# Eight PSUM banks, the input gates and the first head pair's third tile: a change of order at the start of a hybrid decoder step

## The chip, the cores and the metric

The kernel runs on one core of one Trainium2 chip. The metric is device time in microseconds (us), the median of three runs. Engines are named as in the profile: PE (TensorE matmul), PEld (its weight load), DVE (VectorE), ACT (ScalarE), POOL (GpSimd), SP (SyncE, which here issues every transfer; SPq is its queue). L193 is line 193 of the kernel.

## The reference, cut to what matters

One layer of a decoder on 512 prompt tokens and 8x8 sample tokens, 576 columns in all, with 1024 features:

```
h  = rmsnorm(x, norm1_g);  z = h @ w_in          # w_in: 1024 x 5896
li = z[M_I:M_F] + m_i_bias                       # input gate of the mLSTM, 4 heads
lf = log_sigmoid(z[M_F:M_END] + m_f_bias)        # its forget gate
hm = mlstm_chunked(q, k, v, li, lf, ...)         # q, k: conv + silu of z; v, o: z
xm = zr + (prev - zr) * r_mix                    # token shift of the RWKV columns
r, kr, vr = xm[0:512], xm[512:1024], xm[1024:1536]   # then decay, a and gate loras
yr = rwkv7_scan(r, decay, k, v, -kk, kk * a, S0)
x += (gates[0] * (hm @ w_branch_m) + gates[1] * (yr @ w_branch_r)) @ w_out
x += (gelu(conv(h2 @ f_up[:, 0])) * (h2 @ f_up[:, 1])) @ f_down
x += sigmoid(rmsnorm(x) @ ple_gate_w) * (pe @ ple_proj);  y = rmsnorm(x)
```

## The kernel before, in words

Features lie on the 128 partitions, tokens along the free axis; the 576 tokens are worked in two halves (hf 0 and 1) of HF = 288. An output tile of a projection is 128 features x 576 tokens: two PSUM banks, one for each half. Each float32 operand is split into a high and a low part, and each k of the 8 input tiles takes three matmuls (high x high, high x low, low x high), so half an output tile is 24 matmuls of 128x288, all issued at L193. Weights come through `wload` (L158 on) in pieces of four k: SP loads a piece into one of RB = 6 buffers `wr`, ACT casts it (L169, `wh`), DVE subtracts (L170, `wl`) into one of WB = 4 pairs of buffers. A new piece therefore waits for the matmuls of the piece four earlier, and its load for the subtraction of the piece six earlier.

The eight PSUM banks are handed out by tag through `bank`: three "d", two "r", one each of "s", "c", "m". A bank is given out again in turn, and the next user waits until the last reader of the one before is done.

A scheduler orders the instructions of every engine when the kernel is built; each engine then runs its own list strictly in that order. The source's order enters as priority: a step that is written later yields to those before it.

At the start, three tiles of w_in, the `lead` (12 and 13, the RWKV loras, and 0, the r of the first pair), are multiplied with unnormalised x, and their banks are scaled by the first norm's row factors `rsr` (half 0 at L425, half 1 at L429) when they are read out (`evac_pad`, L355). With the factors known, the normalised input is made half by half (`norm_half`: DVE L268, ACT L269, DVE or POOL L270; tiles xa0h to xa7l, sixteen in all). Then come the input and forget gates ("if", L458, 16 matmuls a half because the two parts of the weights lie side by side) and w_in's tile 4, the k of the first pair. What follows is a list of steps, `PLAN`: x, a, d, b, s and c are the stages of one pair of RWKV heads (projections and token shift; decay and matrices; inverses of 16x16 blocks on DVE; chunk matrices; samples; output), m is an mLSTM head, g a gate tile. Step x0 uses tiles 0, 4 and 8; tiles 0 and 4 are there by then, and tile 8, the v of the first pair, is an ordinary `dense` with two banks of tag "d". Before the first step stands `mlstm_rows()`: it reads the gates' banks (ACT L975 and L976, DVE L977 and L978, once for each half), and computes the rows of the mLSTM from them (ACT L979 to L981, DVE L982 to L1017), up to a small matmul at L1020 and transposes at L1024.

Each of r_tile's outputs passes through a buffer `zr` of two; one of the two is first used for a block of zeros, `zscr`, which SP writes to four scratch tensors in DRAM (L547, scr0q to scr1t), so that the second tile that needs a `zr` (tile 8) waits for these transfers. At the very start four matmuls on zeros (L394) run before any input is there; ACT's first copy writes a column of their operand `warm` (L391).

Of the kernel before, what the change touches and what calls it, by code (L numbers as in the profile page):

```python
# [7 lines left out]
F32 = mybir.dt.float32  # L8
# [7 lines left out]
P = 128  # L16
# [6 lines left out]
KD = D // P  # L23
# [4 lines left out]
KSC = 128.0 ** -0.5  # L28
DEC = math.exp(-0.5)

PLAN = "x0 a0 d0 x1 b0 a1 d1 s0 c0 g0 m0 b1 g1 x2 a2 d2 s1 c1 m1 g2 b2 x3 a3 d3 g3 s2 c2 b3 g4 g5 s3 m2 g6 c3 g7 m3 g8 g9 g10 g11 g12 g13 g14 g15".split()


VEC = {}
# [61 lines left out]
def build(tc, nc, I, O):  # L96
    from contextlib import ExitStack

    V, S, G, TE, SY = nc.vector, nc.scalar, nc.gpsimd, nc.tensor, nc.sync
    st0 = ExitStack()  # L100

    def pool(stack, name, bufs=1, space=None, **kw):
        if space is not None:
            kw["space"] = space
        if space is None:
            kw["reuse_waits"] = "tile"
        return stack.enter_context(tc.tile_pool(name=name, bufs=bufs, **kw))

    with st0:
# [8 lines left out]
        def bank(tag="m", name="pm"):  # L118
            if tag == "d" and turn:
                tag = turn[0]  # L120
                turn.append(turn.pop(0))
            return ps.tile([P, 512], F32, tag=tag, name=name, bufs=nbufs[tag])
# [5 lines left out]
        def vcol(name, k=0, rows=P):  # L128
            return vec[0:rows, VEC[name] + k:VEC[name] + k + 1]
# [9 lines left out]
        def pieces(n):  # L139
            return [(k, min(4, n - k)) for k in range(0, n, 4)]  # L140

        def half(hf):
            return slice(hf * HF, (hf + 1) * HF)
# [17 lines left out]
        def wload(src, n, pl=None, tags=("wh", "wl"), bufs=WB, raw=None):  # L161

            rpl, rtag, rbufs = raw or (wp, "wr", RB)
            ws = []
            for k, nk in pieces(n):
                wr = rpl.tile([P, 4, P], F32, tag=rtag, name="wr", bufs=rbufs)
                wh, wl = [(pl or wp).tile([P, 4, P], F32R, tag=t, name=t, bufs=bufs) for t in tags]
                SY.dma_start(wr[:, 0:nk, :], src[:, k:k + nk, :])
                S.copy(wh[:, 0:nk, :], wr[:, 0:nk, :])  # L169
                V.tensor_tensor(wl[:, 0:nk, :], wr[:, 0:nk, :], wh[:, 0:nk, :], ALU.subtract)  # L170
                ws.append((wh, wl))
            return ws
# [11 lines left out]
        def dense_half(pm, ws, xs, hf, ks=None):  # L184
            c = slice(hf * HF, (hf + 1) * HF)
            n = len(xs)
            for k in ks or range(n):
                half_k(pm, ws, xs[k], k, n, c)

        def half_k(pm, ws, x, k, n, c):  # L190
            wh, wl = ws[k // 4]
            for i, (w, a) in enumerate(((wh, x[0]), (wh, x[1]), (wl, x[0]))):
                TE.matmul(pm[:, 0:HF], w[:, k % 4, :], a[:, c], start=k == 0 and i == 0, stop=k == n - 1 and i == 2)  # L193
# [17 lines left out]
        nhalf = cp.tile([P, 1], F32, name="nhalf")  # L211
# [44 lines left out]
        def new_split(pl, tag):  # L256
            return [tuple(pl.tile([P, T], F32R, tag=f"{tag}{k}{a}", name=f"{tag}{k}{a}") for a in "hl") for k in range(KD)]
# [111 lines left out]
        xs1 = new_split(xpool, "xa")  # L369
# [6 lines left out]
        with ExitStack() as stn:  # L376
            npool = pool(stn, "n1")
            acc = npool.tile([P, T], F32, name="acc")
            xt = [npool.tile([P, T], F32, name=f"x{k}") for k in range(KD)]
            raw = [[wp.tile([P, 4, P], F32, tag="wr", name="wr", bufs=RB) for _ in range(2)] for _ in lead]  # L380

            def wdma(i, k):
                SY.dma_start(raw[i][k], I["w_in"][lead[i]][:, 4 * k:4 * k + 4, :])

            def xdma(k, hf):
                SY.dma_start(xt[k][:, half(hf)], I["x"][k][:, half(hf)])


            warm = npool.tile([P, 256], F32, name="warm")
            V.memset(warm, 0.0)  # L390
            S.copy(warm[:, 0:1], nhalf)  # L391
            pm = bank("m")
            for _ in range(4):
                TE.matmul(pm[:, 0:256], warm[:, 0:P], warm, start=True, stop=True)  # L394
            SY.dma_start(vec[:, 0:KD], I["vec"][:, 0:KD])
            xdma(0, 0)
            wdma(0, 0)
            xdma(1, 0)
            xdma(2, 0)
            wdma(0, 1)  # L400
            for k in range(3, KD):
                xdma(k, 0)
            SY.dma_start(cst, I["cst"])
            wdma(1, 0)
            wdma(1, 1)
            for k in range(KD):
                xdma(k, 1)
            SY.dma_start(vec[:, KD:NV], I["vec"][:, KD:NV])
            wdma(2, 0)
            wdma(2, 1)  # L410


            lps = {j: [bank(t, "pd") for t in ts] for j, ts in zip(lead, ("dd", "sc", "rr"))}
            lws = [wsplit(raw[0], KD, npool, ("nh", "nl"), 6)]
            def raw_split(k, hf):
                xh, xl = [npool.tile([P, HF], F32R, tag=t, name=t, bufs=14) for t in ("xrh", "xrl")]
                S.activation(xh, xt[k][:, half(hf)], AF.Copy, scale=vcol("norm1_g", k))
                V.scalar_tensor_tensor(xl, xt[k][:, half(hf)], vcol("norm1_g", k), xh, ALU.mult, ALU.subtract)
                return xh, xl

            xr = []
            for k in range(KD):
                xr.append(raw_split(k, 0))
                add_squares(npool, acc, xt[k], k, 0, G)
            S.copy(rsr[:, half(0)], rms_half(npool, acc, 0, "m"))  # L425
            lws.append(wsplit(raw[1], KD, npool, ("nh", "nl"), 6))
            for k in range(KD):
                add_squares(npool, acc, xt[k], k, 1, G)
            S.copy(rsr[:, half(1)], rms_half(npool, acc, 1, "m"))  # L429
            lws.append(wsplit(raw[2], KD, npool, ("nh", "nl"), 6))  # L430
            for k in range(KD):
                for i, j in enumerate(lead):
                    half_k(lps[j][0], lws[i], xr[k], k, KD, slice(0, HF))
            for k in range(KD):
                xr.append(raw_split(k, 1))
            norm_half(npool, xt, rsr[:, half(0)], 0, "norm1_g", xs1)
            for i, j in enumerate(lead):
                for k in range(KD):
                    half_k(lps[j][1], lws[i], xr[KD + k], k, KD, slice(0, HF))

            w2 = []
            for k in (0, 4):
                wr = wp.tile([P, 4, 64], F32, tag="wr", name="wr", bufs=RB)
                w2.append(npool.tile([P, 4, P], F32R, name=f"wif{k}"))
                SY.dma_start(wr, I["w_if"][:, k:k + 4, :])
                S.copy(w2[-1][:, :, 0:64], wr)
                V.tensor_tensor(w2[-1][:, :, 64:128], wr, w2[-1][:, :, 0:64], ALU.subtract)
            w4 = wload(I["w_in"][4], KD)
            lps["if"] = [bank("d", "pd")]
            lps[4] = [bank("d", "pd")]  # L450
            lps["if"].append(bank("r", "pd"))
            lps[4].append(bank("d", "pd"))
            for hf in range(2):
                if hf:
                    norm_half(npool, xt, rsr[:, half(1)], 1, "norm1_g", xs1)
                for k in range(KD):
                    for i in range(2):
                        TE.matmul(lps["if"][hf][:, 0:HF], w2[k // 4][:, k % 4, :], xs1[k][i][:, half(hf)],  # L458
                                  start=k == 0 and i == 0, stop=k == KD - 1 and i == 1)
                    if hf:  # L460
                        dense_half(lps[4][hf], w4, xs1, hf, (k,))
                if not hf:
                    dense_half(lps[4][hf], w4, xs1, hf)


        rp = pool(stR, "rwkv")
# [11 lines left out]
        m0 = mp.tile([4, NB], F32, name="m0")  # L478
# [478 lines left out]
        s0b = mp.tile([P, 32], F32, name="s0b")  # L957
        V1 = []

        def mlstm_rows():  # L960
            sel = mp.tile([P, 512], F32, tag="zy", name="sel")
            SY.dma_start(sel, I["sel"])
            S.copy(selr, sel)
# [9 lines left out]
            for hf in range(2):  # L973
                c = slice(hf * HF, (hf + 1) * HF)
# [38 lines left out]
            s0 = mp.tile([4, NB], F32, name="s0")  # L1013
# [195 lines left out]
                S.activation(th[:, hf * HF:(hf + 1) * HF], pss[hf][:, 0:HF], AF.Tanh, scale=0.5)  # L1209
            SY.dma_start(d_th[i], th)  # L1210

        mlstm_rows()
        for step in PLAN:
            (rwkv_in, rwkv_prep, rwkv_diag, rwkv_mid, rwkv_smp, rwkv_out, mlstm_head, gate)["xadbscmg".index(step[0])](int(step[1:]))
        SY.dma_start(O["o_shift"], o_shift)
        SY.dma_start(O["o_mconv"], o_mconv)

# [5 lines left out]
        x1 = [rpool.tile([P, T], F32, name=f"res{m}") for m in range(8)]  # L1223
# [44 lines left out]
        with ExitStack() as stw:  # L1268
# [5 lines left out]
            for hf in range(2):  # L1274
                c = slice(hf * HF, (hf + 1) * HF)
# [81 lines left out]
        for g, (j0, nj) in enumerate(GR):  # L1357
# [8 lines left out]
            for m in range(8):  # L1366
                pss = dense(I["f_down"][m, :, j0:j0 + nj, :], acts)
                for hf in range(2):
                    c = slice(hf * HF, (hf + 1) * HF)
# [26 lines left out]
        for hf in range(2):  # L1396
            c = slice(hf * HF, (hf + 1) * HF)
# [122 lines left out]
```

## Time and profile before

| what | value |
|---|---|
| median of the three runs | 1073.62 us (1073.53, 1073.62, 1078.61) |
| the profiled execution | 1070.66 us, of it span 1068.8 us |
| PEld, DVE, ACT, POOL busy | 94%, 73%, 48%, 24% of the span |
| ACT busy from 50 to 60 us | 9.61 of 10 us |
| PE busy from 30 to 40, 40 to 50, 50 to 60 us | 9.14, 8.50, 9.16 of 10 us |
| PE busy from 60 to 120 us | 60 of 60 us |
| transfers over the span | 114.74 MB, 107 GB/s |

A row of the timeline has start, duration, engine, line, operation, output<-input, and in brackets how long the engine was idle before it and what ended that. A matmul's duration contains the pipeline, so matmuls that follow each other start closer together than they last. The rows of waits add up such idle time over the whole execution: total, times, longest.

### The profile page before, as it was taken

What the parts mean: (1) busy time and instruction counts of PE and PEld (TensorE: products, weight loads), DVE (VectorE), ACT (ScalarE), POOL (GpSimd) and SP (SyncE); (2) the same over time, 40 slices, a digit from 0 to 9 for tenths busy, and PEclk for the clock granted to TensorE, in tenths of its full rate; (3) what the DMA queues carried; (4) which work ended last, traced back from release to release, by engine and by line L of the source; (5) the groups of instructions that cost most, each with busy time, mean ns of one, the idle gap of its engine ahead of it and who ended that gap; (6) DMA issues with size and microseconds to landing.
All of it is one profiled execution on the core that took longest, in us unless ns stands there. A gap on an engine that the chain in (4) does not pass through costs nothing.

```text
span 1068.8 us, 23108 instructions
## 1 busy us (share of the span) xinstructions
PE 1045.1 (98%) x8991; PEld 1009.0 (94%) x8991; DVE 777.0 (73%) x1645; ACT 508.8 (48%) x1072; POOL 254.5 (24%) x394
## 2 busy tenths in 40 slices
PE   8899999999999999999999999999999999999996
PEld 7899999999989988999999999999999999999996
DVE  7887657876786676356775799945998569975864
ACT  7684634462553344334343465522565236553822
POOL 7622112221131021001401253200343005410300
PEclk9999999999999999999999999999999999999999
DMA  7243412442342322446850312322233322342513
GB/s 252 95 127 93 108 53 58 103 141 60 88 143 75 81 84 91 143 151 234 263 181 1 116 37 93 110 90 75 85 99 97 102 70 90 94 117 67 165 40 123
DMA packets 90894, 114.74 MB, mean 107 GB/s; under 512 B 35617, under 2 KB 45217, under 8 KB 90785
## 3 DMA queue, kind: packets, MB, share of 16 engines
q1 hardware_dynamic: 90784, 113.27, 34.7%
q8 instruction: 70, 1.15, 0.4%
q14 instruction: 40, 0.32, 0.1%
HBM read 94.79 MB, written 18.45 MB: 106 GB/s over the span
## 4 chain that ended last, share of the span: by engine, by line
PE 90%; DVE 4%; DMA 4%; ACT 1%; issue 1%; SPq 0%; POOLq 0%; DVEq 0%; ACTq 0%
PE pd L193 55%; PE pd L306 20%; PE pm L655 1%; PE pm L1106 1%; PE pm L1136 1%; PE pm L835 1%; PE pm L809 1%; DMA yin<-d_y 1%; PE pm L910 1%; DVE xnf L268 1%; PE pm L917 1%; PE pm L1199 1%; PE pm L775 0%; DMA d_y<-og 0%; DMA wr<-i_w_out 0%
## 5 line engine op out<-in xcount | busy, mean ns | idle before, releaser
L169 ACT CAST wh<-wr 128x512 fp32r<-128x512 f32 (+2 forms) x170 | 101.7, 599 | 173.4 <-PE pd L193 140.7
L170 DVE TENSOR_TENSOR wl<-wr,wh 128x512 fp32r<-128x512 f32 (+2 forms) x170 | 118.8, 702 | 82.4 <-ACT wh L169 80.8
L193 PE MATMUL pd<-actl,wh 128*128 128x288 f32 x384 | 111.9, 295 | 0.0
L193 PE MATMUL pd<-acth,wl 128*128 128x288 f32 x384 | 111.4, 295 | 0.0
L193 PE MATMUL pd<-acth,wh 128*128 128x288 f32 x384 | 110.3, 295 | 0.0
L193 PEld LDWEIGHTS pd<-actl,wh 128*128 128x128 f32 x384 | 71.8, 188 | 0.0
L193 PEld LDWEIGHTS pd<-acth,wl 128*128 128x128 f32 x384 | 71.6, 188 | 0.0
L193 PEld LDWEIGHTS pd<-acth,wh 128*128 128x128 f32 x384 | 71.1, 188 | 0.1
L294 ACT CAST wh<-ws 128x512 fp32r<-128x512 f32 x76 | 47.1, 619 | 48.9 <-PE pd L306 24.8
L295 DVE TENSOR_TENSOR wl<-ws,wh 128x512 fp32r<-128x512 f32 x76 | 58.1, 765 | 8.4 <-ACT wh L294 7.9
L300 POOL TENSOR_TENSOR ws<-wr 128x512 f32<-128x512 f32 x19 | 31.7, 1670 | 96.9 <-DVE wl L295 54.1
L294 ACT CAST wh<-wr 128x512 fp32r<-128x512 f32 x57 | 35.3, 619 | 38.5 <-PE pd L306 24.0
L1333 POOL COPY o_f<-u 128x2 f32<-128x2 f32 x22 | 26.6, 1209 | 110.8 <-DVE u L1330 109.2
L295 DVE TENSOR_TENSOR wl<-wr,wh 128x512 fp32r<-128x512 f32 x57 | 39.5, 693 | 7.3 <-ACT wh L294 7.2
L216 POOL TENSOR_TENSOR rsc<-rsc,nhalf 128x3 f32<-128x3 f32 x8 | 9.3, 1167 | 131.1 <-DVE rsc L235 131.1
L1342 DVE SCALAR_TENSOR_TENSOR y<-u,vec,y 128x592 f32<-128x592 f32 x44 | 38.5, 875 | 1.2 <-ACT y L1340 1.0
L253 ACT ACTIVATE sq<-res 128x288 f32<-128x288 f32 x40 | 17.7, 445 | 36.0 <-DVE res L1279 18.5
L193 PE MATMUL pd<-mgh,ol 128*128 128x288 f32 x112 | 33.0, 296 | 0.0
L193 PE MATMUL pd<-mgl,oh 128*128 128x288 f32 x112 | 33.0, 295 | 0.0
L193 PE MATMUL pd<-mgh,oh 128*128 128x288 f32 x112 | 32.8, 295 | 0.0
L1370 DVE TENSOR_TENSOR res<-res,pd 128x288 f32<-128x288 f32 x48 | 20.9, 450 | 15.7 <-PE pd L193 15.5
L193 PE MATMUL pd<-xa0h,wh 128*128 128x288 f32 x86 | 26.4, 307 | 3.0 <-ACT zr L352 1.6
(825 smaller groups left out, 3949.4 us busy)
## 6 DMA issues: line engine op xcount, KB each, us to landing
wr<-i_w_in SPq DMA_DIRECT2D x92, 256.0 KB
wr<-i_f_up SPq DMA_DIRECT2D x88, 256.0 KB
wr<-i_f_down SPq DMA_DIRECT2D x32, 256.0 KB
d_th<-gst SPq DMA_DIRECT2D x16, 288.0 KB
th<-d_th SPq DMA_DIRECT2D x16, 288.0 KB
wr<-i_w_br SPq DMA_DIRECT2D x16, 256.0 KB
wr<-i_w_out SPq DMA_DIRECT2D x16, 256.0 KB
wr<-i_ple_gate SPq DMA_DIRECT2D x16, 256.0 KB
```

Of the source, the lines that this page charges most:

```text
L169: S.copy(wh[:, 0:nk, :], wr[:, 0:nk, :])
L170: V.tensor_tensor(wl[:, 0:nk, :], wr[:, 0:nk, :], wh[:, 0:nk, :], ALU.subtract)
L193: TE.matmul(pm[:, 0:HF], w[:, k % 4, :], a[:, c], start=k == 0 and i == 0, stop=k == n - 1 and i == 2)
L253: S.activation(sq, x[:, c], AF.Square)
L268: V.scalar_tensor_tensor(xn, xt[k][:, c], vcol(gname, k), rs, ALU.mult, ALU.mult)
L294: S.copy(wh, w)
L295: V.tensor_tensor(wl, w, wh, ALU.subtract)
L300: e.tensor_tensor(t, a, b, ALU.add)
L306: TE.matmul(pm[:, 0:HF], w[a][:, k, :], xs[k][b], start=not more and k == 0 and i == 0, stop=k == 3 and i == 2, skip_group_check=more)
L1333: G.tensor_copy(o_f[:, j, 0:2], u[:, TP:TP + 2])
L1342: V.scalar_tensor_tensor(y, u[:, i:i + 592], w(i), y, ALU.mult, ALU.add)
L1370: V.tensor_tensor(x1[m][:, c], x1[m][:, c], pss[hf][:, 0:HF], ALU.add)
```

## The change

Four edits. The gates' two halves go into banks "s" and "c" (those of lead tile 13) instead of a "d" and an "r". Tile 8 is taken out of step x0's `dense` and put beside tile 4, in the two "r" banks (those of lead tile 0): its first half stands ahead of the second half's norm, its second half is interleaved with the others by k. `mlstm_rows` becomes a step r0, and stands behind x0, a0 and d0 in the plan. ACT's first copy writes to a tile of its own.

```diff
-PLAN = "x0 a0 d0 x1 b0 a1 d1 s0 c0 g0 m0 b1 g1 x2 a2 ... g15".split()
+PLAN = "x0 a0 d0 r0 x1 b0 a1 d1 s0 c0 g0 m0 b1 g1 x2 a2 ... g15".split()
...
-            S.copy(warm[:, 0:1], nhalf)
+            S.copy(npool.tile([P, 1], F32, name="warm1"), nhalf)
...
-            w4 = wload(I["w_in"][4], KD)
-            lps["if"] = [bank("d", "pd")]
-            lps[4] = [bank("d", "pd")]
-            lps["if"].append(bank("r", "pd"))
-            lps[4].append(bank("d", "pd"))
+            more = [4, 8]
+            wm = [wload(I["w_in"][j], KD) for j in more]
+            lps["if"] = [bank("s", "pd"), bank("c", "pd")]
+            lps[4] = [bank("d", "pd") for _ in range(2)]
+            lps[8] = [bank("r", "pd") for _ in range(2)]
...
                     if hf:
-                        dense_half(lps[4][hf], w4, xs1, hf, (k,))
+                        for j, w in zip(more, wm):
+                            dense_half(lps[j][hf], w, xs1, hf, (k,))
                 if not hf:
-                    dense_half(lps[4][hf], w4, xs1, hf)
+                    for j, w in zip(more, wm):
+                        dense_half(lps[j][hf], w, xs1, hf)
...
-        def mlstm_rows():
+        def mlstm_rows(_):
...
-        mlstm_rows()
         for step in PLAN:
-            (rwkv_in, ..., mlstm_head, gate)["xadbscmg".index(step[0])](int(step[1:]))
+            (rwkv_in, ..., mlstm_head, gate, mlstm_rows)["xadbscmgr".index(step[0])](int(step[1:]))
```

The lists of instructions hold the same work on every engine; what differs is their order, in the first 450 us or so. From L464 on line numbers are two higher in the changed kernel, one from L1213 on.

First place: PE, where the second half of the normalised input begins. In the names, pd_538 and pd_540 are the gates' halves, pd_539 and pd_541 tile 4's, pd_829 and pd_830 tile 8's; in the changed kernel pd_551 and pd_552, pd_553 and pd_554, pd_555 and pd_556. Before:

```order
L458 MATMUL pd_540<-xa0h_101,wif0_517 128x288
L193 MATMUL pd_541<-xa0h_101,wh_527 128x288
L193 MATMUL pd_829<-xa0h_101,wh_832 128x288
L193 MATMUL pd_829<-xa0l_102,wh_832 128x288
L193 MATMUL pd_829<-xa0h_101,wl_833 128x288
L193 MATMUL pd_829<-xa1h_103,wh_832 128x288
```

Now:

```order
L193 MATMUL pd_555<-xa7l_116,wh_546 128x288
L193 MATMUL pd_555<-xa7h_115,wl_547 128x288
L193 MATMUL pd_554<-xa0h_101,wh_528 128x288
L458 MATMUL pd_552<-xa0h_101,wif0_518 128x288
L193 MATMUL pd_556<-xa0h_101,wh_540 128x288
L458 MATMUL pd_552<-xa0l_102,wif0_518 128x288
L193 MATMUL pd_554<-xa0l_102,wh_528 128x288
```

Tile 8's first half (pd_829, now pd_555) stood behind the first matmuls of the second half and now stands ahead of them; its second half, which was a block of 24 behind tile 4, is spread among the others.

Second place: ACT, behind the last cast of the normalised input. wh_1148 and wh_1154 (now wh_1149 and wh_1155) are the first and the second piece of the weights of tile 1, the next tile; t1, xgd and xr are the token shifts of the lead tiles, q and k the gates' rows, zr_816 is tile 4's read-out. Before:

```order
L169 CAST wh_1148<-wr_1147 128x512
L516 ACTIVATE t1_681<-rsz_120,dv_666 128x512
L517 ACTIVATE t1_681<-rsz_120,dv_666 128x64
L516 ACTIVATE xgd_700<-zr13_121,dv_666 128x512
L517 ACTIVATE xgd_700<-zr13_121,dv_666 128x64
L975 ACTIVATE q_744<-pd_540,vec_66 4x288
L976 ACTIVATE k_745<-pd_540,vec_66 4x288
L516 ACTIVATE xr_811<-zr0_122,dv_666 128x512
L517 ACTIVATE xr_811<-zr0_122,dv_666 128x64
L352 COPY zr_816<-pd_539 128x288
L352 COPY zr_816<-pd_541 128x224
```

Now:

```order
L169 CAST wh_1149<-wr_1148 128x512
L169 CAST wh_1155<-wr_1154 128x512
L518 ACTIVATE t1_744<-rsz_120,dv_729 128x512
L519 ACTIVATE t1_744<-rsz_120,dv_729 128x64
L518 ACTIVATE xgd_763<-zr13_121,dv_729 128x512
L519 ACTIVATE xgd_763<-zr13_121,dv_729 128x64
L518 ACTIVATE xr_811<-zr0_122,dv_729 128x512
L519 ACTIVATE xr_811<-zr0_122,dv_729 128x64
L352 COPY zr_816<-pd_553 128x288
L352 COPY zr_816<-pd_554 128x224
```

The cast of tile 1's second piece, which stood behind tile 4's read-out, now stands ahead of the token shifts; the gates' second half has moved behind the read-out.

Third place: SP's list of transfers. wr_1932 and wr_1938 (now wr_1933 and wr_1939) are two pieces of the first gate tile's weights; they go into the buffers that tile 1's two pieces leave. Before:

```order
L168 DMA wr_1932<-i_w_in 128x512
L477 DMA sts_660<-i_st_shift 128x112
L568 DMA lr_904<-i_lora_wa 128x256
L855 DMA S0C_1810<-i_st_S 128x512
L547 DMA scr0q_711<-zscr_715 128x585
L547 DMA scr0t_712<-zscr_715 128x585
```

Now:

```order
L168 DMA wr_1933<-i_w_in 128x512
L168 DMA wr_1939<-i_w_in 128x512
L479 DMA sts_723<-i_st_shift 128x112
L570 DMA lr_842<-i_lora_wa 128x256
L857 DMA S0C_1811<-i_st_S 128x512
L549 DMA scr0q_774<-zscr_778 128x585
L549 DMA scr0t_775<-zscr_778 128x585
```

A second piece of weights now stands ahead of the shift states, the lora weights and the four writes of zeros.

More of the change, by code (lines that the diff above doesn't have):

```diff
@@ L29 @@
 DEC = math.exp(-0.5)
-PLAN = "x0 a0 d0 x1 b0 a1 d1 s0 c0 g0 m0 b1 g1 x2 a2 d2 s1 c1 m1 g2 b2 x3 a3 d3 g3 s2 c2 b3 g4 g5 s3 m2 g6 c3 g7 m3 g8 g9 g10 g11 g12 g13 g14 g15".split()
+PLAN = "x0 a0 d0 r0 x1 b0 a1 d1 s0 c0 g0 m0 b1 g1 x2 a2 d2 s1 c1 m1 g2 b2 x3 a3 d3 g3 s2 c2 b3 g4 g5 s3 m2 g6 c3 g7 m3 g8 g9 g10 g11 g12 g13 g14 g15".split()
 VEC = {}
@@ L1210, in gate @@
             SY.dma_start(d_th[i], th)
-        mlstm_rows()
         for step in PLAN:
-            (rwkv_in, rwkv_prep, rwkv_diag, rwkv_mid, rwkv_smp, rwkv_out, mlstm_head, gate)["xadbscmg".index(step[0])](int(step[1:]))
+            (rwkv_in, rwkv_prep, rwkv_diag, rwkv_mid, rwkv_smp, rwkv_out, mlstm_head, gate, mlstm_rows)["xadbscmgr".index(step[0])](int(step[1:]))
         SY.dma_start(O["o_shift"], o_shift)
```

## The prediction, made before the changed kernel was run

> **What bounds the kernel.** I read the page first, then PE's waits, then the timelines of all engines from 30 to 85 us, where the change lies. The page:
>
> ```profile
> span 1068.8 us, 23108 instructions
> PE 1045.1 (98%) x8991; PEld 1009.0 (94%) x8991; DVE 777.0 (73%) x1645; ACT 508.8 (48%) x1072; POOL 254.5 (24%) x394
> PE 90%; DVE 4%; DMA 4%; ACT 1%; issue 1%; SPq 0%; POOLq 0%; DVEq 0%; ACTq 0%
> ```
>
> PE is busy 98% of the span and makes 90% of the chain that ended last. The change alters no matmul, so it can only move the 23.7 us in which PE is not busy. Of PE's waits these bear on it:
>
> ```profile
> PE pd L193 <- ACT zr L352: 1.6, 1, 1.6
> ...
> PE pm L775 <- DMA TT<-scr0t: 1.5, 1, 1.5
> PE pd L193 <- DVE k L978: 1.4, 1, 1.4
> ...
> PE pd L458 <- ACT xa0h L269: 0.2, 1, 0.2
> ```
>
> The timeline of PE places them:
>
> ```profile
> 2.82 3.78 PE L394 MATMUL pm<-warm 128*128 128x256 f32 x8 [2.82 <-ACT warm L391]
> ...
> 12.35 0.61 PE L193 MATMUL pd<-xrl,nh 128*128 128x288 f32 x1 [0.31 <-DVE xrl L418]
> ...
> 32.45 0.30 PE L458 MATMUL pd<-xa0h,wif 128*128 128x288 f32 x1
> ...
> 38.19 0.29 PE L193 MATMUL pd<-xa7h,wl 128*128 128x288 f32 x1
> ...
> 38.99 0.37 PE L193 MATMUL pd<-xa0h,wh 128*128 128x288 f32 x1
> 40.78 0.37 PE L193 MATMUL pd<-xa0h,wh 128*128 128x288 f32 x1 [1.42 <-DVE k L978]
> 40.99 0.30 PE L193 MATMUL pd<-xa0l,wh 128*128 128x288 f32 x1
> ...
> 43.49 0.30 PE L193 MATMUL pd<-xa6h,wl 128*128 128x288 f32 x1
> ...
> 50.84 0.40 PE L193 MATMUL pd<-xa0h,wh 128*128 128x288 f32 x1 [1.56 <-ACT zr L352]
> ...
> 54.14 0.30 PE L193 MATMUL pd<-xa0h,wh 128*128 128x288 f32 x1
> ```
>
> At 40.78 tile 8's first half begins, in the bank that held the gates' first half, when DVE's L978 has read it; at 50.84 its second half, in the bank of tile 4's first half, when ACT has read that. At 54.14 tile 1 begins. Nineteen matmuls from 40.99 to 43.49 give the pitch: 0.1316 us.
>
> **What is removed.** With banks of their own neither wait has a cause, and tile 8's first half (24 matmuls, 3.2 us) fills the time until the second half's xa0h is there. From 32.45 there are 128 matmuls (16.85 us) and about 0.6 for the transposes of the second norm: the first 40 matmuls took until 38.19 + 0.13, 5.87 us where the pitch alone gives 5.26. The second half begins at 41.5, later than every input it had to wait for; lead tile 13's banks, which the gates now take, are read out by 39.7. Tile 1 begins at 49.9 instead of 54.14: 4.2 us won, 3.2 of it listed idle, the rest the slower first matmuls after each wait. This holds as long as those 24 matmuls cover the norm; without them the gates' 0.2 us is the floor.
>
> The copy to a tile of its own lets the matmuls on zeros start some 1.4 us earlier. I cost it at nothing: PE still waits for DVE at 12.35, and everything behind follows from there.
>
> **What is added.** Nothing is computed in addition, but three lists change. These are ACT's rows of before:
>
> ```profile
> 46.16 0.62 ACT L169 CAST wh<-wr 128x512 fp32r<-128x512 f32 x1 [2.60 <-PE pd L193]
> 46.68 0.72 ACT L516 ACTIVATE t<-rsz,dv 128x512 f32<-128x512 f32 x1
> ...
> 48.52 0.49 ACT L975 ACTIVATE q<-pd,vec 4x288 f32<-4x288 f32 x1
> ...
> 49.43 0.70 ACT L516 ACTIVATE xr<-zr,dv 128x512 f32<-128x512 f32 x1
> ...
> 50.38 0.77 ACT L352 COPY zr<-pd 128x288 f32<-128x288 f32 x3
> ...
> 57.36 0.39 ACT L352 COPY zr<-pd 128x288 f32<-128x288 f32 x1
> ...
> 59.21 1.28 ACT L981 ACT_TABLE_LOAD   x1
> 60.50 0.69 ACT L981 ACTIVATE zy<-zy 4x576 f32<-4x576 f32 x1
> ...
> 75.65 0.77 ACT L597 ACTIVATE sq<-xk,vec 128x576 f32<-128x576 f32 x1
> ```
>
> (1) ACT now casts tile 1's second piece right behind its first. With four weight buffers that piece takes the place of tile 4's second, which is free only after the 60th of the 64 matmuls of the second half: 41.5 + 59 x 0.1316 = 49.3, plus half a us for the matmul and the signal, 49.8. ACT runs its list in order, so from 46.1 to 49.8 it stands still, with the token shifts behind it, whose inputs are there. Before, 46.68 to 50.38 held the shifts, and q and k (49.43 - 48.52 = 0.91); without these the read-out of tile 4 comes at 49.8 + 0.52 + 2.79 = 53.1, not 50.38. Tile 1's second half wants that bank at 49.9 + 24 x 0.1316 = 53.1 and has it 0.46 after the copy starts (50.38 to 50.84 before): 0.5 us of wait.
>
> (2) SP sends the second piece of the first gate tile's weights ahead of the shift states and the zeros, and it waits for the subtraction of tile 1's second piece. The rows of DVE, SP and POOL:
>
> ```profile
> 46.81 0.69 DVE L170 TENSOR_TENSOR wl<-wr,wh 128x512 fp32r<-128x512 f32 x1 [2.99 <-ACT wh L169]
> ...
> 56.93 0.46 DVE L533 TENSOR_SCALAR xgd<-xgd 128x576 f32<-128x576 f32 x1 [0.32 <-ACT xgd L532]
> ...
> 61.22 0.75 DVE L982 SCALAR_TENSOR_TENSOR hn<-k,zy 4x576 f32<-4x576 f32 x1 [1.44 <-ACT zy L981]
> ...
> 71.74 1.54 DVE L585 TENSOR_TENSOR_SCAN cs<-rmask,sp 128x128 f32<-128x128 f32 x5
> ...
> 73.79 0.17 DVE L1017 TENSOR_TENSOR s0x<-cst,s 4x32 f32<-4x32 f32 x1
> ```
>
> ```profile
> 47.95 0.38 SPq L477 DMA_DIRECT2D sts<-i_st_shift  x1
> ```
>
> ```profile
> 57.13 0.29 POOL L508 MEMSET zr<- 128x1 f32 x1 [3.62 <-DMA scr1t<-zscr]
> ```
>
> The subtraction that SP waited for ended at 47.50, the new one at 49.8 + 0.62 + 0.7 = 51.1; all that stands behind it in the queue, from sts to the zeros, is 3.6 us later, and the zeros land at 60.7 instead of 57.1.
>
> (3) Tile 8's read-out, at 57.36 before, is 6.98 behind tile 4's. Its list gains q and k (0.91) and a cast (0.52), loses one activation (0.6) and an idle 0.3: 60.6, and with the zeros' landing 60.8. The token shift of xgd just ahead reaches DVE (56.93 before) at 60.6, and PE's lora product (L905) at 61.1. PE is there at 53.6 + 48 x 0.1316 = 59.9: 1.2 us of wait.
>
> (4) Tile 5's second half needs the read-out of tile 1's first, which stands on ACT behind tile 8's, a cast and two activations, some 2.45 us: 63.25, seen by PE at 63.7. PE is there 0.55 after the lora product, at 61.7: 2.0 us.
>
> (5) The gates' rows now stand behind more read-outs: table load at 65.2 (59.21 before), the activation at 66.45, DVE's hn at 67.2 against 61.22. DVE's list from there to the scans cs has one subtraction and two shifts fewer (10.5 becomes 9.1 us), so they begin at 76.3 against 71.74, and s0x comes at 78.35 against 73.79. PE wants it for L1022 after 98 more matmuls and 0.55, at 77.2: 1.4 us.
>
> (6) sq follows the scans on ACT with one copy more: 80.8 against 75.65, done at 81.6. PE wants it 0.25 and 6 matmuls after L1022, at 79.65: 2.0 us. Before, PE did not wait at either:
>
> ```profile
> 77.74 0.28 PE L602 MATMUL pm<-cst,sq 128*128 128x2 f32 x2
> ...
> 79.16 0.38 PE L193 MATMUL pd<-xa4h,wh 128*128 128x288 f32 x1
> ...
> 80.85 0.38 PE L193 MATMUL pd<-xa0h,wh 128*128 128x288 f32 x1
> ```
>
> The small matmuls from 77.74 to 79.16 take 1.4 us, so PE begins the second half of the first gate tile at 83.1, where before it stood at 80.85: **2.25 us later, not 4.2 earlier.** (The five waits make 7.1; the 0.6 that is missing are gaps that before had between 54.14 and 80.85.) By the same reckoning the row factors and matrices that PE wants next are 2 to 3 us ahead of it, and PE runs through.
>
> (7) The rest of the order, to about 450 us, changes too. What PE waits for there are the round trips of the 16x16 inverses through DRAM:
>
> ```profile
> 127.64 1.26 SPq L756 DMA_DIRECT2D TT<-scr0t  x2
> ```
>
> ```profile
> 130.78 0.29 PE L775 MATMUL pm<-TT,X 64*64 64x64 f32 x2
> ```
>
> Pair 0's came just in time. The lists hold 197 large matmuls between the pair's first matrix product and this one before, 182 now: 2.0 us less cover; but TT now goes ahead of Q's two transfers, about 1.3 us. For pair 2, which had the wait of 1.5, cover grows by 8 matmuls, 1.05 us. These nearly cancel: 0, with ends of -1.5 (that wait goes) and +4.0 (15 matmuls of cover lost at pair 0 and at pair 1, none given back).
>
> Sum: 1070.66 + 2.25 = 1072.9 for the profiled execution, which lies 3 us under the median; on the median 1073.62 + 2.25 = **1075.9 us**, a change of 0.2%. Half a per cent, 5.4 us, is about what a measurement of this kernel tells from no change.
>
> **A rule that speaks against the change.** How PE's clock answers to gaps, in two 3.4 us stretches (stretch, length, busy time and count of PE, PEld, DVE, ACT and POOL, granted clock, DMA share, GB/s):
>
> ```profile
> 8.60:12.00 3.40, 2.55 (x11) 1.57 (x10) 3.32 (x5) 3.40 (x11) 2.70 (x3) 1.00 0.99 342
> 12.00:15.40 3.40, 3.09 (x12) 2.72 (x12) 3.40 (x4) 3.39 (x9) 3.28 (x4) 0.55 1.05 342
> ```
>
> After a stretch with 11 matmuls, where 26 fit, the granted clock fell to 0.55 for the next, and 12 matmuls went through. The Trainium skill (TensorE: Matmul & The Clock Gate, Part 1) says that the clock halves after an idle window of about 3.4 us and comes back after a busy one; the trace agrees with the length, and shows it fall after a window that was only thinly filled.
>
> **Rivals.** A: the clock. From 59.9 to 63.7 PE would be idle for 3.2 us and from 77.2 to 81.6 for 3.4. A half-speed stretch costs 14 x 0.1316 = 1.8 us; after the first, waits (5) and (6) cover it, after the second nothing does: 1077.7. Against it: the second gap has 6 matmuls in its middle. B: the waits do not come, because ACT is not held, or its backlog drains before PE needs it; the 4.2 us stay: 1069.4, and 1068.4 with pair 2's gain. For it: ACT is busy 48% overall. Against: its list is fixed, and the cast needs the buffer. C, slower: pairs 0 and 1 lose 15 matmuls of cover each, and their inverses come late by all of it, 4.0 us on top of (1) to (6): 1079.9. It decides once more than 3.1 of the 4.0 are not covered. For it: pair 0 had no slack. Against: TT goes earlier in the queue.
>
> **Numbers.** The forecast 0.50, A 0.16, B 0.20, C 0.14. A and the forecast lie within 0.5%; of B a quarter reaches beyond 1068.25, of C all lies above 1079.0. So faster 0.05, same 0.81, slower 0.14. The range takes in three quarters of B and half of C: 1068.3 to 1079.9.
>
> **What would show it.** Tile 1 begins at 49.9 with no wait of PE from 38 to 50 us. ACT idles 3 to 4 us up to 49.8, ended by PE. The shift states' transfer starts at 51 to 52. PE waits for L352 twice between 53 and 64, for DVE's L535 at 61, and near 78 and 81 for s0x and sq. It is wrong if ACT is not idle there, if the first gate tile's second half begins before 80.8, or if the waits behind 120 us add up to more than 2 us more or less than before.

## The result, and the profile after

| | before | changed |
|---|---|---|
| median (runs) | 1074.07 us (7) | 1085.61 us (7) |
| lowest, highest | 1071.95, 1081.18 | 1083.86, 1089.84 |
| the profiled execution, its span | 1070.66, 1068.8 | 1084.97, 1082.0 |

The changed kernel is slower: 1.0097 of before, 95% interval 1.0075 to 1.012, some 11 us. The forecast was 1075.9, with 1068.3 to 1079.9 as its range. The two profiled executions lie 14.3 us apart, since the one of before is among its fastest; where 2.8 us of that difference belong I don't try to say.

The page of the changed kernel:

```profile
span 1082.0 us, 23101 instructions
PE 1054.2 (97%) x8991; PEld 1014.4 (94%) x8991; DVE 780.3 (72%) x1645; ACT 510.1 (47%) x1072; POOL 255.8 (24%) x394
```

The same 8991 matmuls keep PE busy for 1054.2 us where before it was 1045.1, and PE is not busy for 27.8 us, before 23.7. So of 13.2 us of span 4.1 are idle time, and 9.1 are matmuls that took longer. What makes them longer is the granted clock. Windows of 20 us of the changed kernel, PE alone (stretch, length, busy time, matmuls, granted clock, DMA share, GB/s), the five in which it differs most from before:

```profile
0.00:20.00 20.00, 17.22 (x73) 0.83 0.84 260
...
60.00:80.00 20.00, 15.84 (x112) 1.00 0.30 89
80.00:100.00 20.00, 19.98 (x129) 0.83 0.28 88
...
480.00:500.00 20.00, 15.70 (x97) 0.83 0.63 217
...
540.00:560.00 20.00, 17.63 (x128) 1.00 0.83 270
```

and the same windows of before:

```profile
0.00:20.00 20.00, 16.01 (x72) 0.91 0.86 276
...
60.00:80.00 20.00, 20.00 (x151) 1.00 0.35 112
80.00:100.00 20.00, 20.00 (x162) 1.00 0.32 96
...
480.00:500.00 20.00, 20.00 (x156) 1.00 0.68 228
...
540.00:560.00 20.00, 19.77 (x148) 1.00 0.48 151
```

Three windows have a mean of 0.83: in each, 6.8 of 20 us at half speed, which costs up to 3.4 us. Those at 80 and 480 us make 6.8 of the 9.1. The first window can't be compared by this column. The profile's clock record begins only at 5.1 us in the changed kernel and at 8.9 us in before, and what stands ahead of it is shown as 1.00; but in before the matmuls from 6.64 to 8.32 us follow each other at 0.24 us, nearly twice the pitch of 0.13. What the two starts differ by is the first number of the next table, 0.2 us.

Since the order differs, the two traces can't be compared row by row. I gave every kind of matmul its usual interval, added these up along PE's list, and noted when each kernel had the same amount of matmul work behind it. The changed kernel against before, in us (minus is earlier), by the time in before (another choice of the usual interval moves single positions by up to 1.8 us):

```
time in before       27.7  52.5  73.5  94.0  113.9  479  500  563  1038
changed against it   +0.2  -3.7  -2.3  +4.5   +4.3  +4.3 +12.2 +13.3 +13.5
```

Two places make it: 73 to 94 us, 6.8 us, and 479 to 500 us, 8 us. Between them, where the prediction looked for gains and losses of its own, nothing is left.

**The first place.** PE's waits in the changed kernel:

```profile
PE pm L1161 <- ACT hn L1158: 3.2, 1, 3.2
...
PE pd L193 <- ACT zr L352: 1.5, 1, 1.5
...
PE pm L604 <- ACT sq L599: 1.4, 1, 1.4
PE pm L1022 <- DVE s0x L1019: 1.3, 1, 1.3
...
PE pm L1164 <- DVE og L1162: 0.9, 1, 0.9
```

The timelines of PE, and of ACT, DVE and SP, in the first 83 us:

```profile
50.53 0.30 PE L193 MATMUL pd<-xa0h,wh 128*128 128x288 f32 x1
60.05 0.65 PE L905 MATMUL pm<-xgd,lg 128*128 128x288 f32 x2
62.23 0.40 PE L193 MATMUL pd<-xa0h,wh 128*128 128x288 f32 x1 [1.53 <-ACT zr L352]
77.25 0.40 PE L1022 MATMUL pm<-s0x,cst 4*128 4x32 f32 x2 [1.28 <-DVE s0x L1019]
80.02 2.18 PE L604 MATMUL pm<-cst,sq 128*128 128x2 f32 x10 [1.37 <-ACT sq L599]
82.80 0.59 PE L193 MATMUL pd<-xa0h,wh 128*128 128x288 f32 x1
```

```profile
45.99 1.14 ACT L169 CAST wh<-wr 128x512 fp32r<-128x512 f32 x2 [1.83 <-PE pd L193]
50.33 0.46 ACT L352 COPY zr<-pd 128x224 f32<-128x224 f32 x2 [0.20 <-PE pd L193]
59.49 0.77 ACT L352 COPY zr<-pd 128x288 f32<-128x288 f32 x3 [0.95 <-DMA scr1t<-zscr]
79.19 0.77 ACT L599 ACTIVATE sq<-xk,vec 128x576 f32<-128x576 f32 x1
```

```profile
48.39 0.38 SPq L479 DMA_DIRECT2D sts<-i_st_shift  x1
```

Tile 1 begins at 50.53 (54.14 before), with no wait of PE from 38 us on. Then PE meets what ACT and DVE make: at 62.23 a bank that ACT has not read, at 77.25 the rows' s0x, at 80.02 sq. The second half of the first gate tile begins at 82.80, where before it did at 80.85. And from there the clock counts (stretches of 3.41 us, cut where the clock changes; columns as above):

```profile
76.77:80.18 3.41, 1.56 (x10) 1.00 0.49 149
80.18:83.59 3.41, 3.41 (x17) 0.50 0.21 77
83.59:87.01 3.42, 3.42 (x16) 0.50 0.00 0
87.01:90.42 3.41, 3.41 (x27) 1.00 0.44 146
```

Two waits of 1.3 and 1.4 us stand 2 us apart; behind the second the clock is at a half for 6.8 us.

**The second place** is the last mLSTM head. Its output matrices go to ACT, DVE and POOL for a norm, some 7 us, and PE's transposes need the result. Before:

```profile
472.92 0.33 SPq L941 DMA_DIRECT2D d_y<-bon  x1
483.30 0.26 ACT L1137 COPY hn<-pm 128x129 f32<-128x129 f32 x1
489.66 2.04 ACT L1156 ACTIVATE hn<-hn,hr,hsc 128x128 f32<-128x128 f32 x5 [3.39 <-DVE hr L1154]
```

The changed kernel:

```profile
484.59 0.27 ACT L1139 COPY hn<-pm 128x129 f32<-128x129 f32 x1 [2.34 <-PE pm L1138]
488.30 0.33 SPq L943 DMA_DIRECT2D d_y<-bon  x1
491.92 2.03 ACT L1158 ACTIVATE hn<-hn,hr,hsc 128x128 f32<-128x128 f32 x5 [1.87 <-DVE hr L1156]
492.46 1.63 PE L1161 MATMUL pm<-cst,hn 128*128 128x128 f32 x4 [3.25 <-ACT hn L1158]
494.96 0.45 PE L1164 MATMUL pm<-cst,hn 128*128 128x128 f32 x1 [0.87 <-DVE og L1162]
```

The norm takes 6.4 us from the last copy to hn before, 7.3 now. What PE has to do meanwhile differs: by its rows, 67 large matmuls before (29 of gate tiles, 38 of the branch product, input y), now 31, and none with y. The branch product needs the output of the last RWKV pair, which goes to DRAM at 472.92 before and at 488.30 now (d_y): the pair's output comes 15.4 us later than before, the head's last copy only 1.3. So PE runs dry for 3.25 us, again for 0.87, and the clock is at a half from 493.2 to 500.0.

### The profile page after: what moved, and what is told of

The parts are those of the page before. It is cut to its first block, busy times and chain, and to the rows that moved or that the text cites. A ratio compares the mean times of both kernels' runs of the same rounds, so it can differ in the third digit from the quotient of the medians.

```text
span 1082.0 us, 23101 instructions
## 1 busy us (share of the span) xinstructions
PE 1054.2 (97%) x8991; PEld 1014.4 (94%) x8991; DVE 780.3 (72%) x1645; ACT 510.1 (47%) x1072; POOL 255.8 (24%) x394
## 3 DMA queue, kind: packets, MB, share of 16 engines
q8 instruction: 70, 1.15, 0.4%
## 5 line engine op out<-in xcount | busy, mean ns | idle before, releaser
L254 DVE TENSOR_TENSOR acc<-acc,sq 128x288 f32<-128x288 f32 x42 | 19.0, 456 | 13.0 <-ACT sq L253 12.3
```

What stands on the lines that cost most here:

```text
L254: (eng or V).tensor_tensor(acc[:, c], acc[:, c], sq, ALU.add)
```

## The experiments

Each is compared with before on the same chip; the chips differ between runs, so two runs are best compared by their ratios. The position is the one explained above, against before, in us.

| run | median, us | ratio to before, 95% interval | at 52 | at 114 | at 479 | at 563 |
|---|---|---|---|---|---|---|
| changed | 1085.61 | 1.0097 (1.0075 to 1.012) | -3.7 | +4.3 | +4.3 | +13.3 |
| e1_warm | 1074.00 | 0.9992 (0.9978 to 1.0005) | -0.1 | -0.1 | +0.9 | +1.1 |
| e2_rows | 1074.13 | 0.9994 (0.9977 to 1.001) | -0.9 | -0.4 | +1.7 | +2.7 |
| e3_banks | 1076.84 | 1.0029 (1.0007 to 1.0051) | -3.9 | +0.1 | +2.7 | +4.8 |
| e4_tail | 1072.75 | 0.9989 (0.9973 to 1.0005) | -3.8 | +3.4 | +2.0 | +0.6 |
| e5_sq | 1071.41 | 0.9975 (0.996 to 0.9991) | -4.4 | +3.2 | +0.5 | -1.3 |
| e6_tail_sq | 1077.60 | 1.0035 (1.0019 to 1.0051) | -4.3 | +3.0 | -0.1 | +4.0 |
| e7_before_tail | 1067.72 | 0.9952 (0.9932 to 0.9971) | +0.3 | -0.5 | -0.4 | -3.0 |
| e8_zeros | 1084.05 | 1.0092 (1.0068 to 1.0116) | -3.8 | +3.4 | +2.1 | +11.0 |
| e9_rows_later | 1074.34 | 1.0009 (0.9992 to 1.0026) | -4.1 | +1.8 | +3.7 | +3.2 |
| e10_rows_later_tail | 1074.37 | 1.0006 (0.9989 to 1.0022) | -4.2 | +1.6 | +6.1 | +4.8 |
| e11_head2 | 1080.51 | 1.0059 (1.0033 to 1.0084) | +0.1 | -0.1 | +8.8 | +7.4 |
| e12_banks_tail | 1074.89 | 1.0018 (1.0001 to 1.0035) | -3.8 | +1.9 | +0.7 | +1.2 |
| e13_fill | 1083.01 | 1.0082 (1.0058 to 1.0107) | -3.9 | +3.2 | +1.9 | +12.2 |
| e14_half_fill | 1083.90 | 1.0092 (1.0061 to 1.0122) | -3.6 | +3.7 | +2.3 | +11.4 |

### The change in parts

**e1_warm**, before with the copy alone:

```diff
-            S.copy(warm[:, 0:1], nhalf)
+            S.copy(npool.tile([P, 1], F32, name="warm1"), nhalf)
```

> Before with one edit: ACT's first copy writes a tile of its own, so the four matmuls on zeros need DVE alone. The order of all engines stays as before. Theory: their start moves from 2.8 us to 1.3, the granted clock falls to a half that much earlier and lasts longer before the matmuls come densely, and by 28 us nothing is left of it (in the changed kernel 1.57 earlier at the start, 0.16 later at about 28 us): within 1 us of the kernel before, 1074. Rival: the longer stretch at half clock is a loss of its own, 1.7 us: 1075.8. Second rival: the earlier start stays: 1072.5.

1074.00, ratio 0.9992. The matmuls on zeros start 1.56 us earlier, and at 27.7 us 0.1 is left: the first 28 us take the same time. Nothing won, nothing lost, as forecast.

**e2_rows**, before with the rows' step alone:

```diff
-PLAN = "x0 a0 d0 x1 ...
+PLAN = "x0 a0 d0 r0 x1 ...
...
-        mlstm_rows()
```

> Before with one edit: mlstm_rows() is the step r0 behind d0; banks and tile 8 stay as they were. The order differs only up to about 125 us; the tail of the plan is that of before. Theory (the rows' place makes the waits at s0x and sq, and the half clock behind them): two waits of PE of 1 to 2 us near 75 to 80 us and a stretch of 3 to 7 us at half clock, nothing else: 4 to 7 us slower than before, 1078 to 1081. Rival (the read-outs of tile 8 beside tile 4 make them late, the rows' place alone does nothing): no wait there, within 1 us of before.

1074.13: no wait at s0x or sq, no half clock there. The expectation was wrong, its rival right about the time: the later place of the rows does nothing by itself. PE comes to sq at 78.15, and ACT has done it by 76.8.

**e3_banks**, the changed kernel without the rows' step:

```diff
-PLAN = "x0 a0 d0 r0 x1 ...
+PLAN = "x0 a0 d0 x1 ...
...
+        mlstm_rows(0)
         for step in PLAN:
```

> The changed kernel with one edit taken back: mlstm_rows() is called ahead of all steps again, banks, tile 8 and the copy stay changed. Its order keeps 10 us of matmuls between the last mLSTM head's output matrices and the transposes that need their norm (before 9, changed kernel 4). Theory (rows' place for the waits near 78, the lost cover at the last head for those near 490): neither shows, the 4 us won before 50 us stay, less 1.5 for the wait at ACT's read-out near 62: 1070 to 1073. Rival (banks and tile 8 alone bring the loss): 1080 or more.

1076.84, 3 us slower than before, where 1 to 4 faster was expected. The timelines of PE and ACT:

```profile
77.61 1.28 PE L604 MATMUL pm<-cst,sq 128*128 128x2 f32 x10 [1.77 <-ACT sq L599]
```

```profile
76.80 0.76 ACT L599 ACTIVATE sq<-xk,vec 128x576 f32<-128x576 f32 x1
```

PE goes on with sq at 77.61; before, it did at 77.74. PE's 3.9 us lead ends on the spot: ACT's list, not PE, sets when sq is there, and it starts it 1.15 us later than before (75.65). A half-clock stretch of 3.4 us follows (1.7 us). From +0.1 at 114 us the position goes to +2.7 at 479: waits at the inverses' matmuls (L777; 1.0 us at 133, 1.5 at 213, 1.0 at 378) and another half-clock stretch of 3.4 us from 379.6 us. The last loss, +2.7 to +4.8, is two waits for the sum of the branches, 1.1 us at 544.07 and 1.3 at 546.42, with a third such stretch. Banks and tile 8 alone are no gain, and the rows' step makes the first place worse only together with them.

**e4_tail**, the changed kernel with the last head one place later:

```diff
-... g6 c3 g7 m3 g8 g9 ...
+... g6 c3 g7 g8 m3 g9 ...
```

> The changed kernel with the last mLSTM head one place later in the plan: g7 g8 m3 for g7 m3 g8. The first 270 us and more of its order are those of the changed kernel; from the third head on, matmuls of gate tiles and of the branch product stand between the last head's output matrices and its transposes (9 us of them where the changed kernel has 4). Theory (that cover is what was lost at 480 to 510 us, 8 us with the half clock behind the gap): the waits of 3.2 and 0.9 and the half clock there go, 6 to 8 us faster than the changed kernel: 1077.5 to 1080. Rival (the late chain of the last RWKV pair moves the gap to the gates or the branch product): within 2 us of the changed kernel, 1084 to 1087.

1072.75: 12.9 us below the changed kernel by the medians, 11.6 by the two ratios, more than the 6 to 8 expected. PE has 71 matmuls with y between the last output matrix and the transposes, and the wait there is gone; the position goes from +2.0 to +2.8 at the head, where the changed kernel goes from +4.3 to +12.2. Another 3.3 us of difference come between 500 and 563, where the waits for the branch sum (1.4 and 0.7 in the changed kernel) go.

**e7_before_tail** makes the same edit to before.

> Before with the last mLSTM head one place later (g7 g8 m3). Theory: before had that head covered (8.8 us of matmuls; now 10.7), so the edit that takes 13 us off the changed kernel is worth little here: within 2 us of before. Rival (the place of the head is worth something of its own, not only the cover that the change had taken): 3 us or more faster.

1067.72, 5.8 us faster than before, the fastest of all: the rival. So of the 12.9 us that the edit takes off the changed kernel, not all is cover that the change had taken. With the later head in both kernels the change costs 5.0 us by the medians (1072.75 against 1067.72) and 4.0 by the ratios; with the head in its old place, 11.5 and 10.4. Some 6.5 us of the change's loss thus hang on the place of the last head, and 4 to 5 do not. The trace puts 2.6 of the control's gain behind 479 us (the wait of 1.3 us for VS, which before had, is gone); the two profiled executions are 2.1 us apart, the medians 5.8, and the rest has no place that they show.

### The first place

**e5_sq**, the changed kernel; sq depends only on xk, but stood in the buffer of the scans and behind them:

```diff
             xr, xk, xv = pairs[p]["x"]
+            sq = rp.tile([P, T], F32, name="sq", tag="sqq")
+            S.activation(sq, xk, AF.Square, scale=vcol("r_kk", p))
             lr = ...
...
-            sq = rp.tile([P, T], F32, tag="t2", name="sq")
-            S.activation(sq, xk, AF.Square, scale=vcol("r_kk", p))
```

> The changed kernel with sq (the squares of k, an input that is ready some 23 us before) in a tile of its own and written first in rwkv_prep, not in the tile that the scans leave. Theory (the 4 us won before 50 us are given back where PE meets the chain of ACT and DVE at s0x and sq, and the half clock there comes from those two waits standing close together): the wait at sq goes, the half clock near 80 us goes or shrinks, 2 to 5 us. Its order also has 10 us of matmuls ahead of the last head's transposes, so the loss near 490 us (8) and near 550 us (3) should go too: 1069 to 1074 in all. Rival (PE waits at the next result of the same chain, s0x or nkk, instead): the early part stays as in the changed kernel, 1073 to 1077.

1071.41, in the range. But early it is the rival that holds. PE's waits:

```profile
PE pm L224 <- ACT bc L221: 2.6, 1, 2.6
...
PE pm L582 <- ACT sp L584: 1.5, 1, 1.5
...
PE pm L582 <- DVE xw L530: 1.2, 1, 1.2
```

The wait at sq is gone and three others, 5.3 us, have come, all for ACT and DVE within the same 35 us; behind the last, from 82.2 us, the clock is at a half for 3.4 us. At 114 us the run stands at +3.2. Its gain comes later: 75 matmuls cover the last head.

**e6_tail_sq** has e4's plan in addition.

> The same with the last mLSTM head behind g8 as well. Theory: both heads 2 and 3 have 8 to 11 us of matmuls ahead of their transposes, no wait there; as the former run or 1 us faster, 1068 to 1073. Rival: the later head moves its wait to the branch product or the norm behind it: 1 to 3 us slower than the former.

1077.60, 6 us slower than e5, where the same or 1 us less was expected. At the head nothing is lost (-0.1 at 479, -0.3 at 500); at 543.35 and 545.92 us PE waits 1.3 us for the branch sum and 1.2 for the output weights, and the clock falls (0.91 over 20 us). The rival's place was right, its size too small.

**e8_zeros**, the changed kernel with the zeros in a tile of their own:

```diff
-        zt = rp.tile([P, 585], F32, tag="zr", name="zscr", bufs=2)
+        zt = rp.tile([P, 585], F32, tag="zs", name="zscr")
```

> The changed kernel with the zeros zscr in a tile of their own, so that tile 8's read-out does not wait for the transfers. Its order at the last head is that of the changed kernel, uncovered. Theory (early gains are waited off at s0x and sq): the wait of 1.5 us near 62 us goes and comes back there, so the time stays within 1.5 us of the changed kernel, 1084 to 1087. Rival (each wait is a loss of its own): 1.5 to 2 us faster.

1084.05, 1.6 us less, with intervals that overlap: not told apart by the time. In the trace ACT no longer stops at 59 us, sq starts at 77.84 (79.19 in the changed kernel), PE's wait near 62 us is gone, those at s0x and sq are 1.2 and 1.6. The two waits did not grow by what was saved: the stop had held ACT's own list, and that comes earlier too.

**e9_rows_later** has r0 behind x1, in the changed kernel.

```diff
-PLAN = "x0 a0 d0 r0 x1 b0 ...
+PLAN = "x0 a0 d0 x1 r0 b0 ...
```

> The changed kernel with r0 one step later still, behind x1. In its order the matmuls on s0x stand 25 places behind those on sq, and the last head has 10 and 3.4 us of matmuls ahead of its transposes (changed kernel 4.2 and 0). Theory (at 76 to 80 us PE meets the end of a chain on ACT and DVE in which the rows' twenty small steps stand; two waits so close make the clock fall): with the rows behind it sq comes 2 to 4 us earlier, the waits there shrink to under 1 us in all, no half clock near 80 us; at 100 us it is 3 to 5 us ahead of the changed kernel, and the tail's 8 to 11 us go too: 1069 to 1073. Rival (the chain of ACT is full without the rows, as the run with sq ahead suggests, where the waits only moved): the early part stays 3 to 5 us behind before: 1073 to 1077.

1074.34, the rival's time. No wait at s0x, and PE goes on with sq at 76.92, 3.1 us earlier than in the changed kernel, but after 1.2 us of wait; at 79.98 it waits 1.8 us for ACT's read-out of a gate tile (L1211), and the clock falls (0.91 over 80 to 100 us). So again the wait moves on to the next result of ACT, and at 114 us the run stands at +1.8. The last head is covered; waits of 1.0 and 2.0 us for an inverse's transfer (L777, 214 and 374 us), with half clock for 6.8 us behind the second, lose part of that.

**e10_rows_later_tail** adds the later head.

> The same with the last mLSTM head behind g8. Theory: as e7_before_tail gained 5.8 us on before, this gains some 3 to 6 on the former run: 1066 to 1070. Rival (the late head moves its wait to the branch products near 545 us, as with sq ahead, where it cost 6): 1075 or more.

1074.37, no gain. Neither expectation fits: no wait above 0.5 us near 550, but the same waits at L1211 and L777, and half clock between 360 and 400 us (0.89 and 0.85).

**e12_banks_tail** is e3_banks with the later head.

> The kernel of e3_banks (gates and tile 8 in banks of their own, rows early) with the last head behind g8. Theory (the banks and tile 8 alone are worth nothing once PE meets ACT's chain near 77 us; the late head is worth 3 to 6 us): 1070 to 1074, 3 to 6 us slower than e7_before_tail. Rival (the banks' 4 us are won in the end where no later wait takes them back): 1064 to 1068.

1074.89, 7 us slower than e7_before_tail: a little beyond the theory, and against the rival.

### The second place

**e11_head2**, an injection into before:

```diff
-... b3 g4 g5 s3 m2 g6 c3 g7 m3 g8 ...
+... b3 g4 g5 g6 g7 s3 m2 c3 m3 g8 ...
```

> Before with the plan's third part written g6 g7 s3 m2 c3 m3 g8 for s3 m2 g6 c3 g7 m3 g8, which leaves the third mLSTM head (m2) 0.3 us of matmuls ahead of its transposes and 0.1 between them and the next use (before 7.1 and 2.2), while the last head keeps 9.5 and 3.4. Banks, tile 8 and rows as before. Theory (an uncovered head costs its chain of norms, some 8 us from the last output matrix to the transposes, and a half clock behind the gap): PE waits 6 to 8 us at the transposes near 400 us, 1.7 to 3.4 us more by the clock: 8 to 11 us slower than before, 1081 to 1085. Rival (the loss at the last head came of something else there, as the branch product's loads): within 3 us of before.

1080.51, 7.8 us slower, close below the range, but at another place than named. PE's waits:

```profile
PE pm L835 <- DVE MT L839: 2.4, 1, 2.4
...
PE pm L845 <- DVE MT L839: 1.4, 1, 1.4
```

and its windows there:

```profile
400.00:420.00 20.00, 16.21 (x213) 0.87 0.13 43
420.00:440.00 20.00, 19.94 (x124) 0.71 0.16 57
```

The gates that went ahead are missing at the last pair's matrices; at head 2's transposes PE doesn't wait. The position goes from -0.2 at 327 us to +10.2 at 436: 3.8 us of waits in a stretch without large matmuls, and 8.4 us of clock. That shows the kind of loss, not the head's.

**e13_fill** and **e14_half_fill**, the changed kernel with four, or two, matmuls more for h == 3, whose result is thrown away (the transposes overwrite it):

```diff
             pm = bank()
+            for _ in range(4 if h == 3 else 0):
+                TE.matmul(pm[:, 0:256], og[:, 0:P], og[:, 0:256], start=True, stop=True)
             for w in range(4):
                 TE.transpose(pm[:, w * P:(w + 1) * P], hn[:, w, 0:P], ident)
```

> The changed kernel with four matmuls more (128x256, float32, some 0.8 us each by the four on zeros at the start) ahead of the last head's transposes, written to the bank that these overwrite. PE's order is that of the changed kernel up to them, and the transposes still need the norm that comes at 492 us. Theory (of the 8 us lost there 3.4 are the clock, which falls for 6.8 us because of the gap): the transposes begin when they did, the granted clock stays at 1 behind them, and the time is 3 to 4 us below the changed kernel, 1081 to 1083, though PE has 3.2 us more to do. Rival (the clock falls for a reason of its own, or the matmuls delay what follows): the same as the changed kernel or up to 3 us more, 1085 to 1089.

> The same with two such matmuls, which leave some 1.7 us of the gap and the 0.9 behind the transposes. Theory (one short wait, as those of 1.4 and 1.6 us at 41 and 51 us in before, is borne): the clock stays, 1081 to 1083. Rival (what counts is the work in a stretch of 3.4 us, and a stretch of transposes and waits is too thin): it falls for 3.4 us, 1083 to 1086.

1083.01 and 1083.90, 2.6 and 1.7 less than the changed kernel, with intervals that overlap its own; the first lies at the edge of the theory's range, the second in the rival's. In the traces the theory of e13 does not hold. The four took 1.9 us, not 3.2 (those on zeros, from which the 0.8 us came, stand ahead of the first clock record); the wait at the transposes fell from 3.25 to 1.06 us, and the clock fell all the same. PE's stretches there in e13_fill, cut where the clock changes:

```profile
489.13:492.54 3.41, 2.02 (x10) 1.00 0.93 307
492.54:495.95 3.41, 2.59 (x10) 0.50 1.00 314
495.95:499.37 3.42, 3.42 (x16) 0.50 1.02 388
```

In e14_half_fill, where the wait is 1.92 us, the clock falls as well (0.83 over 480 to 500 us). Ahead of the fall in e13 stand the wait of 1.06 us, the four transposes and the beginning of a wait of 0.87; 2.02 us of work in 3.41 were not enough. But the profiled execution of e13 is the slowest of its six (1085.96 us, mean granted clock 0.984; the other five have 0.988 to 0.991), and its clock falls once more, at 554 us for 6.8 us, where the changed kernel's does not. Whether it fell at the head in the other five is not shown. So the clock's share of the loss at the head is read from the trace, and no run shows it by itself; a filler that lasts until the branch product is there was not tried.

## Why the prediction was wrong, step by step

- **What is removed**: right. 3.6 us won at tile 1 (50.53), 4.2 forecast, and no wait from 38 to 50 us. The copy on zeros: nothing, by e1.
- **(1)** wrong: ACT stands still 1.83 us, up to 45.99, not to 49.8. The second piece's cast runs right behind the first, from 46.5 us, and cannot then be in the place of tile 4's second piece, which PE reads until 50. Tile 8's second piece is read as long, so by elimination it took the place of tile 8's first, whose last matmul ends by 46.44. Here the buffers were not given out in turn. No wait at 53 us.
- **(2)** half right: SP is held by 0.4 us, not 3.6 (48.39 against 47.95), but the zeros land at 59.49, 2.4 later: the last of them was issued only 0.45 us later (51.24 against 50.79), so the transfers themselves took some 1.9 us longer. Why is not shown; 256 KB of weights more stand ahead of them.
- **(3)** wrong: PE comes to L905 at 60.05 and doesn't wait. **(4)** right in place, 1.53 for 2.0 us.
- **(5), (6)** right: 1.28 and 1.37 us at s0x and sq, for 1.4 and 2.0.
- The mark: the first gate tile's second half was put at 83.1 and began at 82.80. That is 1.95 us later than before, for a forecast of 2.25, with two of five waits not there and 1.3 us of half clock already in it. That it came within 0.3 us is luck: the waits make 4.2 us where 7.1 were forecast, and the half clock and a lead that is 0.6 smaller fill most of the difference.
- **The clock (rival A, 0.16)** came, and larger: 3.4 us, not 1.8, for two half-speed stretches in a row. The argument against it, that six matmuls stand in the gap's middle, did not hold: with them PE was busy for 1.56 of the 3.41 us ahead of the fall, and that was thin enough. The clock fell again at 493 us, a place that the prediction does not consider. The rule quoted in the prediction (the Trainium skill, TensorE: Matmul & The Clock Gate, Part 1) speaks of an idle window; here the clock fell after a stretch that was 46% filled.
- **(7), the step that failed.** It took the lists to differ up to about 450 us and netted the rest to 0. They differ to 555 us, and the largest single loss, 8 us, lies at 479 to 500: 4.1 us of waits and 6.8 us at half clock. The lists showed it before any run: 31 large matmuls for 67 between the last head's output and its transposes. I had counted cover only for the round trips of the inverses. Those came out near 0, as said (+4.3 at 114 us and at 479).
- **Rival C** had the kind (cover lost in the order) and the wrong place; B did not come.

That the tail is the larger part is shown by e4 and e7 together: their one edit takes some 6.5 us more off the changed kernel than off before, of the 10.4 to 11.5 that the change costs, while the first place still stands at +3.4. That PE's early lead ends at ACT's list is shown by e3, and the waits that move on in e5 and e9 agree: in all eleven kernels with the new banks PE is 3.6 to 4.4 us ahead at 52 us, and in none is it ahead at 114. Why the scheduler puts the last pair further back is not shown; e2 and e3, with half of the change each, keep the head covered.

## What to carry to other kernels

A gain of PE ahead of a point at which it meets another engine's list is worth only the slack that it has there: write down when that engine's result was ready in the profile before (here 76.4 us, for a use at 77.74) before counting it. Where a scheduler makes the order, an edit at 40 us moves work at 490; count for every chain between two uses of PE what stands beside it, up to the last row that differs. And price a gap on PE with the clock behind it: 2.7 us of waits near 78 us and 4.1 near 493 cost 6.8 and 7.9.

## What the runs showed of the hardware

The half-speed stretches last 3.4 us or a multiple of it: 6.8 us in the changed kernel, 10 from 375.6 us in e10_rows_later_tail, 17 from 414.7 us in e11_head2. In each trace all changes of the clock lie whole multiples of 3.413 us apart; in the changed kernel they stand at 8.50, 15.33, 80.18, 87.01, 493.19 and 500.02 us. The clock thus changes on a fixed raster, and the raster lies elsewhere in each trace. One stretch of it in the changed kernel, ahead of the fall at 493 us:

```profile
489.78:493.19 3.41, 0.66 (x2) 1.00 0.82 218
```

and two in before, with its waits of 1.4 and 1.6 us:

```profile
39.65:43.06 3.41, 2.28 (x17) 1.00 0.02 5
49.89:53.30 3.41, 2.46 (x18) 1.00 0.96 299
```

The raster splits each of those two waits, the stretches keep 2.28 and 2.46 us of work, and the clock stayed at 1. Over all sixteen traces, from the first clock record on, every stretch at full speed with less than 1.8 us of work was followed by half speed, of those with 1.8 to 2.7 us some were, and above that only the four named next. So the same wait need not cost the same: e3_banks and e12_banks_tail wait 1.77 and 1.76 us at sq, and the half clock behind it lasts 3.4 us in the one and 6.8 in the other. That the place of the raster decides this fits the numbers; no run varies it alone.

e1_warm has a half-speed stretch that no idle time precedes. PE's windows:

```profile
309.00:312.40 3.40, 3.40 (x52) 1.00 0.30 83
312.40:315.80 3.40, 3.40 (x25) 0.50 0.83 243
315.80:319.20 3.40, 3.40 (x53) 1.00 0.40 143
```

PE is listed as busy throughout; in the 3.41 us ahead of the fall stand 50 matmuls, 32 of them 32x32 (the inverses, L789). e2_rows, e7_before_tail and e11_head2 have the same at 312 to 314 us, before has not. Records that say busy are thus no proof that the clock sees enough work.
